# Interleaving the blocks of single experts with the blocks of paired experts in the last stage of a two-layer decoder trunk

## The chip, the cores and the metric

The kernel runs on one core of one Trainium2 chip. The metric is the device time of one execution in microseconds (us). The median of three runs of the kernel before is 1392.48 us (1391.92 to 1393.53).

## The reference, cut to what matters

The kernel computes two decoder layers over 256 tokens of width 1024. The change touches only the last part of the second layer, a mixture of eight experts of which each token uses two:

```python
logits = (x2d @ router).astype(F32)
top_val, top_exp = lax.top_k(logits, 2)          # two of eight experts for each token
gates = jax.nn.softmax(top_val, axis=-1)
...
# for each expert e, on the rows xb of the tokens that chose it:
(jax.nn.silu(xb @ w1[e]) * (xb @ w3[e])) @ w2[e]    # w1, w3: 1024 x 3584, w2: 3584 x 1024, float32
...
# each token sums its two experts' rows times their gates, and then
x = layer_norm(alpha * x + moe(x), ln2_g, ln2_b)
```

The weights of the eight experts are 8 x 3 x 1024 x 3584 floats, 352.3 MB, and each is read from HBM once.

## The kernel before, in words

Up to about 475 us the kernel does the first layer, the attention of the second and the routing. What follows is the stage of the experts, written by `swiglu` from a list of items. The experts are sorted by how many tokens chose them. The first four places (0 to 3) have 128 token slots each and run alone. The last four (4 to 7) have 64 slots each and run in pairs, (4, 5) and (6, 7), the two experts side by side in the two 64-column halves of TensorE.

An item is a block of 512 of the 3584 hidden columns. There are seven items for an expert that runs alone and seven for a pair. An item does the product with w1 (`up` or `up2`), SiLU on ScalarE (line 699), the product with w3, the multiplication of the two on VectorE (line 710), then a transposition (`gate_T`) and the product with w2 (`down`), which is issued in the middle of the next item: after its w1 product and before its w3 product.

- An alone item reads six loads of 1 MB (two each for w1, w3, w2). Each 128x1024 half of a load is split by ScalarE (line 222, `hi`) and VectorE (line 223, `lo`) into two fp32r parts, and each product is three matmuls of 512 columns (`mm3`, lines 232 to 234): 72 matmuls in an item. Five pairs of `hi` and `lo` tiles exist (`WB=5`).
- A pair item reads twelve loads of 1 MB and feeds the raw float32 words to TensorE (line 285 in `up2`, line 650 in `down`). It has no split. The trace has 96 matmul records for an item: 64 for w1 and w3, 32 for w2.

All loads are issued by SyncE's queue (SPq, line 218) in program order, into eleven slots of 1 MB that are used in rotation (`raw()`, the list `late`). A load waits until the readers of the load that had its slot before are done: the VectorE split for an alone item, the matmuls for a pair item. So transfers run at most eleven loads ahead of their use.

The order of the blocks is that of `order` at line 1069: expert 0 alone (seven items), the pair (6, 7), expert 1, expert 2, the pair (4, 5), expert 3. Before an expert's first item its token rows are gathered with one-hot matmuls (`gather` for places that run alone, `gather2` for a pair); places 1 and 2 share one gather. After an expert's last item `combine` (lines 1051 and 1038) scales the result by the gates on ScalarE and VectorE and adds it to the token rows with eight matmuls into `zacc`, four PSUM banks that hold the sums of all tokens for the whole stage. `residual` (line 862) puts alpha times the stage's input into these banks in the third item. PSUM has eight banks here, four tagged `acc` and four tagged `wk`; as `zacc` holds the four `acc` banks, the accumulator of the running expert (`e_acc`, line 1033) holds two of the `wk` banks, and two are left.

`overflow` (line 881) is a branch for experts with more tokens than slots. It is not taken on these inputs, but every engine passes its test, at the second item of place 2. The last item is cut in two of 256 columns.

Of the kernel before, what the change touches and what calls it, by code (L numbers as in the profile page):

```python
# [7 lines left out]
F32 = mybir.dt.float32  # L8
# [5 lines left out]
ALU = mybir.AluOpType  # L14
# [138 lines left out]
def trunk(ctx: ExitStack, tc: tile.TileContext, a, out, R=6, WB=5, NF=16):  # L153
# [60 lines left out]
    def load(w, r0, nr, c0, ncol):  # L214
        t = raw()
        v = t[:, :nr * ncol].rearrange("p (k f) -> p k f", k=nr)
        src = w.at(r0, nr, c0, ncol)
        nc.sync.dma_start(v if len(src.shape) == 3 else t[:, :nr * ncol], src)
        return v
# [70 lines left out]
    def run(*gens):  # L290
        for g in gens:
            yield from g
# [5 lines left out]
    def end(g):  # L298
        for _ in g:
            pass  # L300
# [312 lines left out]

    x1, sta, rest, (behind, _) = finish_ln(accs, x0, g1, b1)

    def swiglu(items, ws, between=None, behind=None, next_ws=None, tail=False):

        def gate_T(it, g):  # L620
            n = it[4]
            if isinstance(it[0], tuple):
                pt, t = wk(), fa("gt")
                for j in range(n // P):
                    TE.transpose(pt[:, j * P:(j + 1) * P], g[0][:, j * P:(j + 1) * P], ident)  # L625
                A.copy(t[:, :n], pt[:, :n])  # L626
                return t
            gs = []
            for q in g:
                pt = wk()  # L630
                for j in range(n // P):
                    TE.transpose(pt[:, j * P:(j + 1) * P], q[:, j * P:(j + 1) * P], ident)  # L632
                gh, gl = fb("gh"), fb("gl")
                A.activation(gh[:, :n], pt[:, :n], AF.Copy)  # L634
                V.tensor_sub(gl[:, :n], pt[:, :n], gh[:, :n].bitcast(F32))  # L635
                gs.append((gh, gl))
            return gs

        def down(it, gs, fill=iter(())):
            w1, w3, w2, c0, n, sta, accs, first, last, pre, post = it  # L640
            nr = n // P
            accs = accs()
            if isinstance(w1, tuple):
                for r in range(0, nr, 2):
                    ws = [load(w, c0 // P + r, 2, 0, D) for w in w2]
                    for j in range(2):
                        for d in range(2):
                            for i, w in enumerate(ws):
                                s = slice((r + j) * P + i * 64, (r + j) * P + (i + 1) * 64)
                                TE.matmul(accs[0][d][i * 64:(i + 1) * 64, :], lhsT=gs[:, s],  # L650
                                          rhs=w[:, j, d * 512:(d + 1) * 512], start=first and r + j == 0,
                                          stop=last and r + j == nr - 1)
                            step(fill)
                end(fill)
                if post:
                    post()
                return
            for r in range(0, nr, 2) if not last else [0]:
                ws = []
                m = 1 if tail and it is items[-1] else 2  # L660
                for q in range(r, nr if last else r + 2, m):
                    v = load(w2, c0 // P + q, m, 0, D)
                    ws += [split(v[:, j:j + 1, :]) for j in range(m)]
                for i, (gh, gl) in enumerate(gs):
                    for d in range(2):
                        for j, (wh, wl) in enumerate(ws):
                            s = slice((r + j) * P, (r + j + 1) * P)
                            c = slice(d * 512, (d + 1) * 512)
                            mm3(accs[i][d], gh[:, s], gl[:, s], wh[:, 0, c], wl[:, 0, c],
                                first and r + j == 0, last and r + j == nr - 1)  # L670
                            step(fill)
            end(fill)
            if post:
                post()

        prev = after = None
        for it in items:
            if it is items[-1] and next_ws:
                after = next_ws()
            w1, w3, w2, c0, n, sta, accs, first, last, pre, post = it  # L680
            fill = pre() if pre else None
            if fill:
                if prev:
                    step(fill, 3)
                    down(prev[0], gate_T(*prev), fill)
                    prev = None
                else:
                    end(fill)
            sta = sta()
            p1 = [wk() for _ in sta]  # L690
            two = isinstance(w1, tuple)
            u = up2(p1[0], w1, c0, n, sta[0]) if two else up(p1, w1, c0, n, sta, ws, between)
            step(u, 2)
            if prev:
                gs = gate_T(*prev)
            end(u)
            s = [fa("sl") for _ in sta]
            for q, p in zip(s, p1):
                A.activation(q[:, :n], p[:, :n], AF.Silu)  # L699
            held = tail and it is items[-1]  # L700
            if prev and not held:
                down(prev[0], gs)
            p3 = [wk() for _ in sta]
            with tc.issue_after(behind) if ws else nullcontext():
                end(up2(p3[0], w3, c0, n, sta[0]) if two else up(p3, w3, c0, n, sta))
            ws = None
            if held:
                down(prev[0], gs)
            for q, p in zip(s, p3):
                V.tensor_mul(q[:, :n], q[:, :n], p[:, :n])  # L710
            prev = (it, s)
        down(prev[0], gate_T(*prev))
        return after and after + next_ws(4)


# [111 lines left out]
    with tc.issue_after(behind):  # L827
# [13 lines left out]
        for h in range(2):  # L841
# [15 lines left out]
            A.activation(t[:, :, 0], gs, AF.Copy)  # L857
            V.tensor_sub(t[:, :, 1], gs, t[:, :, 0].bitcast(F32))
            gg.append(t)
    zacc = [[acc(), acc()] for h in range(2)]  # L860

    def residual():

        identr = fb("identr")[:, :P]
        A.activation(identr, ident, AF.Copy)
        for h in range(2):
            for d in range(2):
                v = x3[:, h, d * 512:(d + 1) * 512]
                hi, lo = fb("xa"), fb("xb")
                A.activation(hi, v, AF.Copy, scale=ALPHA)  # L870
                V.scalar_tensor_tensor(lo, v, ALPHA, hi.bitcast(F32), op0=ALU.mult, op1=ALU.subtract)
                TE.matmul(zacc[h][d], lhsT=identr, rhs=hi, start=True, stop=False)
                TE.matmul(zacc[h][d], lhsT=identr, rhs=lo, start=False, stop=False)

    iota = cst[:, C_IOTA:C_IOTA + P]

# [155 lines left out]

    def e_acc(e):
        if ("acc", e) not in state:
            state["acc", e] = [[wk(), wk()]]
        return state["acc", e]

    def add_up(ys, ot, gs, y, last=False):

        for d in range(2):  # L1040
            c = slice(d * 512, (d + 1) * 512)
            p = ys[d]
            yh, yl = y[:, 0, c], y[:, 1, c]
            A.activation(yh, p, AF.Copy, scale=gs)
            V.scalar_tensor_tensor(yl, p, gs, yh.bitcast(F32), op0=ALU.mult, op1=ALU.subtract)
            for h in range(2):
                s = slice(h * P, (h + 1) * P)
                TE.matmul(zacc[h][d], lhsT=ot[:, s], rhs=yh, start=False, stop=False)  # L1048
                TE.matmul(zacc[h][d], lhsT=ot[:, s], rhs=yl, start=False, stop=last)  # L1049

    def combine(e, last):
        add_up(state["acc", e][0], *state["ot", e], new_y(), last)
# [12 lines left out]

        return [Picked(n, a[n], ROWS[n], at) for n in ("odd_w1", "odd_w3", "odd_w2")]

    items = []
    order = [[0], [6, 7], [1, 2], [2], [4, 5], [3]]
    for j, qs in enumerate(order):  # L1070
        q = qs[0]
        ch = [(c, 512) for c in range(0, D_FFE, 512)]
        if j == len(order) - 1:
            ch[-1:] = [(D_FFE - 512, 256), (D_FFE - 256, 256)]
        ws3 = list(zip(picked(q), picked(q + 1))) if CAP[q] == 64 else picked(q)
        for i, (c, n) in enumerate(ch):
            first, last = i == 0, i == len(ch) - 1
            pre = None
            if first:
                pre = (lambda qs=qs: end(begin(qs))) if q == 2 else lambda qs=qs: begin(qs)  # L1080
            elif (j, i) == (0, 2):
                pre = residual
            elif (j, i) == (3, 1):
                pre = overflow
            items.append((*ws3, c, n, lambda q=q: state["sta", q], lambda q=q: e_acc(q), first, last, pre,
                          (lambda q=q, l=j == len(order) - 1: combine(q, l)) if last else None))
    swiglu(items, ws, behind=behind, tail=True)


    xo = xp.tile([P, 2, D], F32, tag="x", name="xo", bufs=2)  # L1090
# [52 lines left out]
```

## Time and profile before

| What | Before |
|---|---|
| median of three runs | 1392.48 us |
| the profiled execution, its time | 1392.84 us |
| the profiled execution, span from first to last instruction | 1391.2 us |
| TensorE busy over the span | 1301.0 us (94%) |
| VectorE, ScalarE busy | 774.4 us (56%), 618.0 us (44%) |
| bytes read from HBM | 424.03 MB, 306 GB/s over the span |
| granted TensorE clock, mean | 0.986 |

Times in the rows below are microseconds from the start of the span. In a table of stretches each engine has its busy time and, in brackets, the number of its instructions; PEclk is the granted share of TensorE's full clock, and "DMA share" the mean busy share of the sixteen DMA engines. In a timeline the bracket at the end is the idle time of the engine before the row and what ended it. TensorE's busy time is modelled from pipelined matmuls, so a busy TensorE is not always one at full rate: the number of matmuls in a stretch tells more.

### The profile page before, as it was taken

The numbers are of one execution on the slowest core, as the hardware profiler recorded it, in microseconds if no ns is written. First come the engines' busy times: TensorE is split into PE (matmuls) and PEld (weight loads), VectorE is DVE, ScalarE is ACT, GpSimd is POOL, SyncE is SP. The second block draws the span as 40 slices with busy tenths as digits, with TensorE's granted clock in tenths as the row PEclk, the third lists the DMA queues.
The fourth block names the chain that finished last, engine by engine and source line by source line (L and its number), as shares of the span: only waits on it lengthen the run. The fifth ranks groups of instructions, "written<-read, shape, count | busy, mean of one in ns | idle before, by whom it ended". The sixth has DMA issues, their size and how long they took to land. (4 is left out here: it accounts for less than half of the span.)

```text
span 1391.2 us, 16679 instructions
## 1 busy us (share of the span) xinstructions
PE 1301.0 (94%) x6082; PEld 889.5 (64%) x6082; DVE 774.4 (56%) x1190; ACT 618.0 (44%) x866; POOL 53.7 (4%) x40
## 2 busy tenths in 40 slices
PE   9998999999999899999888999989999978799996
PEld 7766888887777788843222378868884322237885
DVE  6987445558777599800000188878882000008897
ACT  5564444534554388710000177777771000007774
POOL 0022000101023000000000000000000000000001
PEclk9999999999999799999999999999999999999998
DMA  9532455645336389969999999979997999999981
GB/s 368 189 124 110 137 202 215 216 178 181 124 149 257 133 336 365 373 280 420 422 421 421 421 421 420 382 279 383 369 371 296 421 421 421 421 421 421 419 300 48
DMA packets 65403, 426.26 MB, mean 306 GB/s; under 512 B 7840, under 2 KB 12192, under 8 KB 15392
## 3 DMA queue, kind: packets, MB, share of 16 engines
q1 hardware_dynamic: 64304, 421.70, 77.1%
q0 software_dynamic: 864, 3.15, 0.6%
q8 instruction: 50, 0.82, 0.2%
q14 instruction: 41, 0.34, 0.1%
q10 hardware_dynamic: 144, 0.26, 0.1%
HBM read 424.03 MB, written 1.05 MB: 306 GB/s over the span
## 5 line engine op out<-in xcount | busy, mean ns | idle before, releaser
L223 DVE TENSOR_TENSOR lo<-raw,hi 128x1024 fp32r<-128x1024 f32 (+2 forms) x462 | 535.2, 1200 | 135.9 <-ACT hi L222 131.1
L222 ACT ACTIVATE hi<-raw 128x1024 fp32r<-128x1024 f32 (+2 forms) x480 | 468.7, 1021 | 189.8 <-PE wk L234 95.0
L285 PE MATMUL wk<-raw,xg 128*64 128x512 f32 x896 | 217.2, 597 | 30.9 <-DMA raw<-in_odd_w 30.9
L710 DVE TENSOR_TENSOR sl<-sl,wk 128x512 f32<-128x512 f32 (+1 forms) x55 | 36.3, 666 | 346.1 <-PE wk L285 318.9
L232 PE MATMUL wk<-hi,xg 128*128 128x512 f32 (+1 forms) x464 | 180.2, 388 | 4.4 <-DVEq L886 4.4
L233 PE MATMUL wk<-lo,xg 128*128 128x512 f32 (+1 forms) x464 | 181.4, 391 | 0.4 <-DVE lo L223 0.4
L234 PE MATMUL wk<-hi,xg 128*128 128x512 f32 (+1 forms) x464 | 179.0, 386 | 0.0
L285 PEld LDWEIGHTS wk<-raw,xg 128*64 128x64 f32 x896 | 66.0, 136 | 157.9 <-issue 101.4
L650 PE MATMUL wk<-raw,gt 128*64 128x512 f32 x448 | 133.5, 602 | 10.1 <-DMA raw<-in_odd_w 8.7
L626 ACT COPY gt<-wk 128x512 f32<-128x512 f32 x14 | 8.2, 585 | 229.0 <-PE wk L625 229.0
L232 PEld LDWEIGHTS wk<-hi,xg 128*128 128x128 f32 x464 | 88.2, 190 | 22.1 <-issue 4.8
L233 PEld LDWEIGHTS wk<-lo,xg 128*128 128x128 f32 x464 | 88.2, 190 | 20.8 <-DVE lo L223 2.2
L234 PEld LDWEIGHTS wk<-hi,xg 128*128 128x128 f32 x464 | 88.2, 190 | 16.6
L699 ACT ACTIVATE sl<-wk 128x512 f32<-128x512 f32 (+1 forms) x55 | 32.0, 582 | 146.7 <-PE wk L285 104.3
L650 PEld LDWEIGHTS wk<-raw,gt 128*64 128x64 f32 x448 | 40.4, 136 | 81.4 <-issue 52.2
L233 PE MATMUL wk<-lo,gh 128*128 128x512 f32 x224 | 87.4, 391 | 0.7 <-DVE lo L223 0.7
L234 PE MATMUL wk<-hi,gl 128*128 128x512 f32 x224 | 87.4, 390 | 0.4 <-DVE gl L635 0.4
L232 PE MATMUL wk<-hi,gh 128*128 128x512 f32 x224 | 82.0, 393 | 0.6 <-ACT gh L634 0.6
L232 PE MATMUL wk<-hi,xT 128*128 128x512 f32 (+1 forms) x192 | 72.3, 377 | 0.3 <-ACT xT L315 0.3
L233 PE MATMUL wk<-lo,xT 128*128 128x512 f32 (+1 forms) x192 | 71.6, 373 | 0.0
L234 PE MATMUL wk<-hi,xT 128*128 128x512 f32 (+1 forms) x192 | 71.5, 373 | 0.0
L232 PE MATMUL acc<-hi,xT 128*128 128x512 f32 (+1 forms) x172 | 68.9, 401 | 0.9 <-ACT xT L315 0.9
(209 smaller groups left out, 1482.7 us busy)
## 6 DMA issues: line engine op xcount, KB each, us to landing
raw<-in_odd_w SPq DMA_DIRECT2D x331, 1024.0 KB, 13.3
raw<-in_even_w SPq DMA_DIRECT2D x31, 1024.0 KB, 4.8
raw<-in_odd_w_in SPq DMA_DIRECT2D x12, 1024.0 KB, 4.8
raw<-in_even_w_in SPq DMA_DIRECT2D x8, 1024.0 KB, 11.9
raw<-in_odd_w SPq DMA_DIRECT2D x10, 512.0 KB, 4.5
raw<-in_even_w_out SPq DMA_DIRECT2D x4, 1024.0 KB, 5.1
raw<-in_odd_w_out SPq DMA_DIRECT2D x4, 1024.0 KB, 4.7
raw<-in_even_w SPq DMA_DIRECT2D x4, 512.0 KB, 3.2
```

The costliest lines, as they stand in the source:

```text
L222: A.activation(hi, v, AF.Copy)
L223: by.tensor_sub(lo, v, hi.bitcast(F32))
L232: TE.matmul(o, lhsT=sh, rhs=wh, start=first, stop=False)
L233: TE.matmul(o, lhsT=sh, rhs=wl, start=False, stop=False)
L234: TE.matmul(o, lhsT=sl, rhs=wh, start=False, stop=last)
L285: TE.matmul(o[i * 64:(i + 1) * 64, :ncol], lhsT=sta(r + k, i), rhs=v[:, k, :], start=r + k == 0, stop=r + k == KT - 1)
L626: A.copy(t[:, :n], pt[:, :n])
L650: TE.matmul(accs[0][d][i * 64:(i + 1) * 64, :], lhsT=gs[:, s], rhs=w[:, j, d * 512:(d + 1) * 512], start=first and r + j == 0, stop=last a ...
L699: A.activation(q[:, :n], p[:, :n], AF.Silu)
L710: V.tensor_mul(q[:, :n], q[:, :n], p[:, :n])
```

## The change

The order of the items is new. The items of the four experts that run alone (28) form one list, those of the two pairs another, first (4, 5), then (6, 7), and the new list takes two of the first and one of the second in turn. Pair items are thus items 3, 6, 9 and so on; the cut item at the end is now that of the pair (6, 7). Each place that runs alone has its own gather. Two experts' accumulators are open at the same time; they take the four `acc` banks, and all four `wk` banks are free for products.

The tokens' sums are no longer in PSUM. `residual` scales the stage's input `x3` in place, with two ScalarE instructions, and a `combine` that is not the last makes its eight matmuls into `wk` banks and adds these to `x3` with four VectorE instructions. In the last product with w2 a new generator `sums` opens four banks (two `acc`, two `wk`) and puts `x3` into them with four float32 matmuls by the identity, and the last `combine` adds to these banks. The final normalization reads them as before. For a pair item that is the very last, `down` loads w2 in pieces of 0.5 MB.

```diff
-    def swiglu(items, ws, between=None, behind=None, next_ws=None, tail=False):
+    def swiglu(items, ws, between=None, behind=None, next_ws=None, tail=None):
...
             if isinstance(w1, tuple):
-                for r in range(0, nr, 2):
-                    ws = [load(w, c0 // P + r, 2, 0, D) for w in w2]
-                    for j in range(2):
+                m = 1 if tail and it is items[-1] else 2
+                for r in range(0, nr, m):
+                    ws = [load(w, c0 // P + r, m, 0, D) for w in w2]
+                    for j in range(m):
...
-        down(prev[0], gate_T(*prev))
+        down(prev[0], gate_T(*prev), *([tail()] if tail else []))
...
-    zacc = [[acc(), acc()] for h in range(2)]
 
     def residual():
 
-        identr = fb("identr")[:, :P]
-        A.activation(identr, ident, AF.Copy)
+        for h in range(2):
+            A.activation(x3[:, h, :], x3[:, h, :], AF.Copy, scale=ALPHA)
+
+    zacc = []
+
+    def sums():
+
+        zacc.extend([[acc(), acc()], [wk(), wk()]])
         for h in range(2):
             for d in range(2):
-                v = x3[:, h, d * 512:(d + 1) * 512]
-                hi, lo = fb("xa"), fb("xb")
-                A.activation(hi, v, AF.Copy, scale=ALPHA)
-                V.scalar_tensor_tensor(lo, v, ALPHA, hi.bitcast(F32), op0=ALU.mult, op1=ALU.subtract)
-                TE.matmul(zacc[h][d], lhsT=identr, rhs=hi, start=True, stop=False)
-                TE.matmul(zacc[h][d], lhsT=identr, rhs=lo, start=False, stop=False)
+                TE.matmul(zacc[h][d], lhsT=ident, rhs=x3[:, h, d * 512:(d + 1) * 512], start=True, stop=False)
+                yield
...
-            state["acc", e] = [[wk(), wk()]]
+            state["acc", e] = [[acc(), acc()]]
...
-                TE.matmul(zacc[h][d], lhsT=ot[:, s], rhs=yh, start=False, stop=False)
-                TE.matmul(zacc[h][d], lhsT=ot[:, s], rhs=yl, start=False, stop=last)
+                ps = zacc[h][d] if last else wk()
+                TE.matmul(ps, lhsT=ot[:, s], rhs=yh, start=not last, stop=False)
+                TE.matmul(ps, lhsT=ot[:, s], rhs=yl, start=False, stop=True)
+                if not last:
+                    V.tensor_add(x3[:, h, c], x3[:, h, c], ps)
...
-    items = []
-    order = [[0], [6, 7], [1, 2], [2], [4, 5], [3]]
-    for j, qs in enumerate(order):
-        q = qs[0]
+
+    def expert(q):
+        end_ = q == 6
         ch = [(c, 512) for c in range(0, D_FFE, 512)]
-        if j == len(order) - 1:
+        if end_:
             ch[-1:] = [(D_FFE - 512, 256), (D_FFE - 256, 256)]
...
             if first:
-                pre = (lambda qs=qs: end(begin(qs))) if q == 2 else lambda qs=qs: begin(qs)
-            elif (j, i) == (0, 2):
+                pre = lambda: begin([q])
+            elif (q, i) == (0, 1):
                 pre = residual
-            elif (j, i) == (3, 1):
+            elif (q, i) == (2, 2):
                 pre = overflow
...
+    alone, paired = run(*(expert(q) for q in range(4))), run(expert(4), expert(6))
+    items = []
+    for it in alone:
+        items += [it, next(alone), next(paired)]
+    items += paired
+    swiglu(items, ws, behind=behind, tail=sums)
```

## Rows read from the trace of the kernel before

**Rows 1.** The page: GB/s in 40 slices of the span.

```profile
GB/s 368 189 124 110 137 202 215 216 178 181 124 149 257 133 336 365 373 280 420 422 421 421 421 421 420 382 279 383 369 371 296 421 421 421 421 421 421 419 300 48
```

**Rows 2.** Stretches: length, engines' busy times, PEclk, DMA share, GB/s.

```profile
480.00:600.00 120.00, 119.34 (x553) 97.78 (x551) 103.36 (x105) 89.19 (x98) 0.00 (x0) 1.00 0.88 332
...
605.00:775.00 170.00, 145.77 (x626) 49.65 (x622) 5.61 (x11) 8.28 (x14) 0.00 (x0) 1.00 1.01 421
800.00:875.00 75.00, 74.60 (x332) 60.36 (x331) 66.07 (x63) 57.34 (x65) 0.00 (x0) 1.00 1.01 420
...
480.00:1360.00 880.00, 821.18 (x3631) 505.66 (x3630) 429.90 (x440) 376.22 (x435) 0.00 (x0) 1.00 0.96 383
```

**Rows 3.** Timeline of VectorE: multiplications of three alone items (start, duration).

```profile
484.19 0.68 DVE L710 TENSOR_TENSOR sl<-sl,wk 128x512 f32<-128x512 f32 x1
...
846.73 0.69 DVE L710 TENSOR_TENSOR sl<-sl,wk 128x512 f32<-128x512 f32 x1 [1.28 <-PE wk L234]
...
863.69 0.69 DVE L710 TENSOR_TENSOR sl<-sl,wk 128x512 f32<-128x512 f32 x1 [1.28 <-PE wk L234]
```

**Rows 4.** The same for the first four items of the first pair.

```profile
614.13 0.69 DVE L710 TENSOR_TENSOR sl<-sl,wk 128x512 f32<-128x512 f32 x1 [15.65 <-PE wk L285]
635.50 0.69 DVE L710 TENSOR_TENSOR sl<-sl,wk 128x512 f32<-128x512 f32 x1 [20.68 <-PE wk L285]
662.50 0.69 DVE L710 TENSOR_TENSOR sl<-sl,wk 128x512 f32<-128x512 f32 x1 [26.31 <-PE wk L285]
692.41 0.69 DVE L710 TENSOR_TENSOR sl<-sl,wk 128x512 f32<-128x512 f32 x1 [29.23 <-PE wk L285]
```

**Rows 5.** Waits from 430 or 475 us on: total us, times, longest.

```profile
SPq L218 <- DVE lo L223: 389.5, 155, 16.5
...
PE wk L285 <- DMA raw<-in_odd_w: 30.9, 24, 1.3
```

**Rows 6.** Loads of the experts' weights: count, size, median us to landing.

```profile
raw<-in_odd_w SPq DMA_DIRECT2D x331, 1024.0 KB, 13.3
...
raw<-in_odd_w SPq DMA_DIRECT2D x10, 512.0 KB, 4.5
```

**Rows 7.** Groups by line from 440 us on: the splits, busy us, mean ns.

```profile
L223 DVE TENSOR_TENSOR lo<-raw,hi 128x1024 fp32r<-128x1024 f32 x324 | 377.6, 1219 | 36.3 <-ACT hi L222 31.8 <-DVEq L886 3.8
L222 ACT ACTIVATE hi<-raw 128x1024 fp32r<-128x1024 f32 x325 | 324.3, 1053 | 43.4 <-PE wk L234 33.6 <-PE acc L234 7.4 <-DVE lo L223 1.5
```

**Rows 8.** Timeline of TensorE where w2 of a pair and a gather alternate.

```profile
788.35 1.08 PE L650 MATMUL wk<-raw,gt 128*64 128x512 f32 x4
...
789.36 0.74 PE L974 MATMUL wk<-oneh,xT 128*128 128x256 f32 x4
...
790.03 1.08 PE L650 MATMUL wk<-raw,gt 128*64 128x512 f32 x4
```

**Rows 9.** VectorE, from expert 2's last item to a pair's first.

```profile
1042.65 0.69 DVE L710 TENSOR_TENSOR sl<-sl,wk 128x512 f32<-128x512 f32 x1 [1.98 <-PE wk L234]
...
1070.57 0.69 DVE L710 TENSOR_TENSOR sl<-sl,wk 128x512 f32<-128x512 f32 x1 [15.65 <-PE wk L285]
```

**Rows 10.** VectorE, expert 1 to expert 2, then past the branch.

```profile
915.18 0.69 DVE L710 TENSOR_TENSOR sl<-sl,wk 128x512 f32<-128x512 f32 x1 [0.60 <-PE wk L234]
...
934.07 0.69 DVE L710 TENSOR_TENSOR sl<-sl,wk 128x512 f32<-128x512 f32 x1 [0.73 <-PE wk L234]
...
957.13 0.69 DVE L710 TENSOR_TENSOR sl<-sl,wk 128x512 f32<-128x512 f32 x1 [2.35 <-PE wk L234]
```

**Rows 11.** From a pair's multiplication to its w2 product; the last combine's first step.

```profile
782.02 0.69 DVE L710 TENSOR_TENSOR sl<-sl,wk 128x512 f32<-128x512 f32 x1 [8.77 <-PE wk L285]
...
784.15 1.07 PE L650 MATMUL wk<-raw,gt 128*64 128x512 f32 x2 [0.73 <-ACT gt L626]
...
1377.28 1.37 ACT L1044 ACTIVATE y<-wk,gs 128x512 fp32r<-128x512 f32 x2 [3.01 <-PE wk L234]
```

**Rows 12.** A stretch with the 0.5 MB loads.

```profile
1352.00:1354.00 2.00, 2.00 (x14) 1.80 (x13) 1.39 (x4) 1.27 (x2) 0.00 (x0) 1.00 0.94 291
```

More of the change, by code (lines that the diff above doesn't have):

```diff
@@ L1079, in trunk @@
             if first:
-                pre = (lambda qs=qs: end(begin(qs))) if q == 2 else lambda qs=qs: begin(qs)
-            elif (j, i) == (0, 2):
+                pre = lambda: begin([q])
+            elif (q, i) == (0, 1):
                 pre = residual
-            elif (j, i) == (3, 1):
+            elif (q, i) == (2, 2):
                 pre = overflow
-            items.append((*ws3, c, n, lambda q=q: state["sta", q], lambda q=q: e_acc(q), first, last, pre,
-                          (lambda q=q, l=j == len(order) - 1: combine(q, l)) if last else None))
-    swiglu(items, ws, behind=behind, tail=True)
+            yield (*ws3, c, n, lambda: state["sta", q], lambda: e_acc(q), first, last, pre,
+                   (lambda: combine(q, end_)) if last else None)
+    alone, paired = run(*(expert(q) for q in range(4))), run(expert(4), expert(6))
[4 more added lines that the diff above has]
+    swiglu(items, ws, behind=behind, tail=sums)
     xo = xp.tile([P, 2, D], F32, tag="x", name="xo", bufs=2)
```

## The prediction

> **What bounds the kernel now.** I read the page's GB/s line first [rows 1]: in the stage of the experts (slices 14 to 39) it alternates between plateaus at 421 and stretches of 270 to 380. The table of stretches says why [rows 2]. In the pair stage (605 to 775) transfers run at 421 GB/s with a DMA share of 1.01, while TensorE has 626 matmul records in 170 us, 3.7 per us. In the alone stages it is the other way: from 480 to 600 TensorE is busy 119.3 of 120 us, and transfers make only 332 GB/s. So the two kinds of item have different limits, and each stage leaves idle what the other lacks. Over 480 to 1360 us transfers average 383 GB/s.
>
> The items' cadence gives the sizes. An alone item takes 16.96 us (863.69 - 846.73 [rows 3]), of which 72 matmuls at 75 us / 332 = 0.226 us (800 to 875 [rows 2]) are 16.3; its six loads, 6.29 MB, are 14.9 us of transfer at 421. A pair item takes 21.4 us as long as its data are there (first to second multiplication [rows 4]); its twelve loads, 12.58 MB, take 29.9 us, and that is the cadence after a few items (third to fourth [rows 4]). Two alone and one pair item together: TensorE 2 x 16.9 + 21.4 = 55.2 us, transfers 25.17 MB / 421 = 59.8 us. The whole stage is 331 loads of 1 MB and 10 of half that [rows 6], 352.3 MB or 837 us at 421, and TensorE's 14 groups are 773 us and its extras: nearly equal totals, which now lie partly one behind the other.
>
> What keeps them from overlapping today is the reach of eleven slots: SyncE's queue waits 389.5 us for splits to free a slot, and TensorE waits for loads in the pair stages [rows 5]. In the first pair stage, items one and two keep 21.4 us and the third loses 5.6 [rows 4]. By the third multiplication, 662.5, two items and the eight w1 and w3 loads of the third are used, 33.6 MB, and 421 GB/s from 605 on gave 24.2 MB: the lead was 9.4 MB, 22 us of transfer. That is short against a block of seven pair items, but long against one.
>
> **The change part by part.** I sum TensorE's path, from the first alone item's multiplication at 484.2 us [rows 3], where both orders are alike, to the end, and then test it against the transfers.
>
> (1) Items. 27 more alone items x 16.9 = 456 us; 13 pair items x 21.4 = 278; the two halves of the cut one 21. What is removed is the waiting of the pair items: some 8.5 us (29.9 - 21.4) in five items of each block.
>
> (2) Changes of form. TensorE now goes between 128-column fp32r and 64-column float32 work about eight times in three items, where a pair item has two today (its transposition). The row that shows one: four pair records take 1.01 us and four 256-column gather matmuls 0.67 us until the next kind starts [rows 8]; at 0.2155 us per 512 columns they would be 0.86 and 0.43, so two changes cost 0.39 us. Six more changes in each of 14 groups at 0.2 us are 17 us. The Trainium skill, "TensorEngine Tiling (Array Packing)", Key Properties, says against this change that switching the tiling mode drains TensorE; it has no price, and rows 8 are what such a drain costs here.
>
> (3) Gathers and combines. The step from an alone expert to a pair took 27.9 us [rows 9]. Its w2 product with transposition (5.9) and the pair's w1 and w3 (64 records, 13.8) are 19.7 of it; the rest, with 0.7 lost in the item before, is 8.9 us for a gather and a combine. A combine between two alone experts cost 18.9 - 17.0 = 1.9 us [rows 10]; I take 2.5 (bounds 1.9 and 3.4) and 5.5 for a gather with its slot matrix. Behind the anchor there are now five gathers (four before: places 1 and 2 shared one), 27.5 us, and five combines ahead of the tail, 12.5. The branch costs 23.1 - 17.0 = 6.1 us [rows 10], as before. Together 46 us.
>
> (4) Sums in SBUF. The eight matmuls of a combine stay. New are four VectorE additions of 128x512, 0.69 us each by the multiplication of that shape [rows 3], 2.8 us in each of five combines; each waits for two matmuls, and behind it on VectorE wait the splits. An alone item has 12 splits of 1.22 us [rows 7] and two smaller steps, 16.0 us in 16.9, so there is little room, but five split pairs are in stock. Bounds 0 and 14 us; I take 3, because pair items give VectorE its room back. As `x3` stays in use, one buffer instead of two is left for `y`; combines lie an item or more apart, so the matmuls that hold it are done and it costs nothing, or one combine's 2.5 us where two experts end in one group. `residual` loses eight matmuls and four VectorE steps that lie behind the anchor; counting it at 0 is safe, as its two ScalarE scalings of 1.05 us [rows 7] fit beside TensorE.
>
> (5) Waits at seams. Where an alone piece follows a pair piece, its first split may not be ready: ScalarE 1.05 and VectorE 1.22 us [rows 7], 2.3 us, at three such seams in each group, 42 in all. Bounds 0 and 96 us. Between alone items, where splits run ahead, an item takes 16.96 us against 72 x 0.226 + 0.5 = 16.8, so 0.1 to 0.2 us is lost; ScalarE and VectorE idle in the pair stages (8.3 and 5.6 us of 170 [rows 2]), so splits should be ahead here too. I take 0.1 us, 4 us.
>
> (6) Tail. After the last multiplication come the way to the w2 product (2.1 us in a whole item [rows 11], 1.5 in a half one), 16 records x 0.2155 = 3.4 us, and the four identity matmuls of `sums`. No such float32 matmul is in the trace; between a fp32r one (0.226) and the four records of a float32 pair that fill the same array (0.86) I take the upper, 3.4 us. From the last combine's first step to the end it stays 1391.2 - 1377.3 = 13.9 us [rows 11], and 0.6 for a change of form.
>
> Sum: 484 + 456 + 278 + 21 + 17 + 46 + 3 + 4 + 1.5 + 3.4 + 3.4 + 0.6 + 13.9 = 1332 us. I round down by 2, as the first items after the anchor ran at 16.8 us: 1330 of span. The profiled execution was 1.6 us longer than its span and 0.4 above the median, so 1331 us.
>
> **Do the transfers keep up?** From 480 to 1360 us 880 x 0.383 = 337.0 MB moved [rows 2], nearly all that was left. At 421 that is 800 us. The first two items and a gather leave the slots full and cost some 9 us; the pieces of 0.5 MB at the end (20, 10.5 MB) move at 291 to 421 [rows 12], up to 10 us more. So transfers end at 1290 to 1300, 30 us ahead of the end, and alone would give about 1315. The lead, 22 us of transfer at the first pair, falls by 59.8 - 55.2 - 1.2 = 3.4 us a group, and gathers, combines and the branch refill it. Before the seventh pair it is thinnest: 22 - 6 x 3.4 + 8 (expert 1's gather and combine) = 9.6 us. Within a group the pair's three pieces draw 6.5 us, so 3 us are left. TensorE paces, narrowly.
>
> **The rivals.** (A) Seams cost about 0.8 us each, a third of what they can: 42 x 0.8 = 34 instead of 4, thus 1361. For it: two streams share five split pairs and two in-order engines, and SiLU and the copies of a pair stand in the same queues. Against it: before, the splits ran ahead past just such steps.
>
> (B) Slower. ScalarE and VectorE are kept in the order in which the items are written: the splits for an alone w2 product stand behind the pair item's SiLU, which waits for its w1 matmuls, and those for w1 and w3 behind its copy and multiplication. Then each of the 42 seams shows the full 2.3 us: 96 instead of 4, thus 1423. From 1.6 us a seam on ((1391 - 1326) / 42) the change loses. Speaking against: TensorE's pace of 0.226 us holds over whole alone stages.
>
> (C) Transfers pace: TensorE's extras hide in the wait for data, 1315 as worked out above.
>
> (D) It gains nothing. Either the lead is worth less than 22 us, and each of the 14 pair items still waits 4.3 us more (60 us), or transfers do not hold 421 for 800 us: 383 GB/s, today's mean, gives 880 us and 1391. Against both: 420 and 421 held in a pair and in an alone stage [rows 2]. The Trainium skill, "SBUF — State Buffer", Summary, would have HBM transfers counted at about 358 GB/s; by that the 337 MB take 941 us, and the end is past 1430. Rows 2 show 421 for 170 us on end, so I give it next to nothing.
>
> **How the numbers follow.** Forecast (1318 to 1345) 55%, A (1345 to 1385) 21%, C (1305 to 1318) 12%, B 7%, D 5%. The forecast is the likeliest: 1331. From 1312 on, most of C is in; up to 1366, the nearer half of A: together a little over 8 in 10. A difference of 0.2%, 2.8 us, is about what a measurement tells from none. Faster: all of the forecast and of C, A, a part of D: 0.89. Same: 0.04. Slower: B, with a little of D: 0.07.
>
> **What would show it.** In stretches of 60 us between 500 and 1280, both sides should be full: DMA share near 1.0 and some 250 matmul records. From every third multiplication to the next it should be 56 to 58 us; TensorE's wait for loads (30.9 us at line 285 now [rows 5]) should nearly go. If a group takes 59.8 us and the share is 1.01 all through, C holds. If TensorE idles behind line 223 or 222 at the seams, it is A or B, by its length. If it still idles for loads with the share below 1, the lead is too short (D). The prediction falls if the cadence of alone or pair items is not 16.9 and 21.4 when they are mixed.

## The result and the profile after

The change takes 1378.46 us, the median of four runs (1374.65 to 1378.92), against 1392.33 before: a ratio of 0.9893 (95% interval 0.9874 to 0.9912). It is faster by 1%, 14 us where 61 were forecast, and outside the range. The profiled execution is the fastest of the four, 1374.65 us with a span of 1372.9.

The page of after, GB/s in 40 slices, and two stretches of it (columns as in [rows 2]): the first group of two alone items and a pair item, from one pair's multiplication to the next, and a later one.

```profile
GB/s 371 193 101 103 166 184 218 221 194 162 155 151 176 170 308 396 422 420 421 412 375 421 419 420 409 381 362 226 420 421 412 405 411 344 421 415 418 394 234 167
...
525.00:581.00 56.00, 56.00 (x253) 34.50 (x253) 29.41 (x27) 28.04 (x30) 0.00 (x0) 1.00 0.99 409
1033.00:1094.00 61.00, 57.98 (x253) 35.15 (x252) 30.97 (x30) 26.66 (x30) 0.00 (x0) 1.00 1.01 412
```

The valleys of [rows 1] are mostly gone (the deepest left, 226, lies at the branch), and the pair's waits for data too. TensorE's list of waits for loads at line 285 had 30.9 us on matmuls (PE, [rows 5]) and this on weight loads (PEld):

```profile
PEld wk L285 <- DMA raw<-in_odd_w: 53.6, 33, 2.2
```

Of the loads of the experts only the first row below is left in it; the others are the loads' own waits for slots:

```profile
PEld wk L285 <- DMA raw<-in_odd_w: 2.0, 6, 0.4
...
SPq L218 <- DVE lo L223: 337.3, 132, 11.6
SPq L218 <- PE wk L285: 221.4, 73, 10.3
SPq L218 <- PE acc L651: 104.3, 26, 8.9
```

So the change does what it says: pairs and singles share the transfers. But the two groups above hold the same 253 matmul records, and the first takes 56.0 us with TensorE never idle, the second 61.0 with 3.0 us idle; the other 2.0 us stand in records that the model of busy time draws out. The granted clock is 1.00 in both. The multiplications on VectorE (start, duration) show where. The first two rows bound the first group, the last four are a later one:

```profile
525.12 0.69 DVE L711 TENSOR_TENSOR sl<-sl,wk 128x512 f32<-128x512 f32 x1 [12.37 <-PE wk L285]
...
581.11 0.69 DVE L711 TENSOR_TENSOR sl<-sl,wk 128x512 f32<-128x512 f32 x1 [8.13 <-PE wk L285]
...
1032.76 0.69 DVE L711 TENSOR_TENSOR sl<-sl,wk 128x512 f32<-128x512 f32 x1 [9.03 <-PE wk L285]
1052.90 0.69 DVE L711 TENSOR_TENSOR sl<-sl,wk 128x512 f32<-128x512 f32 x1 [5.39 <-PE wk L234]
1069.89 0.69 DVE L711 TENSOR_TENSOR sl<-sl,wk 128x512 f32<-128x512 f32 x1 [2.44 <-PE wk L234]
1093.76 0.69 DVE L711 TENSOR_TENSOR sl<-sl,wk 128x512 f32<-128x512 f32 x1 [9.06 <-PE wk L285]
```

From pair to pair it is 56.0 us at first (forecast 56.4), and 61.0 in later groups that hold no gather, combine or branch, called steady below: 20.1 for the alone item behind the pair, 17.0 for the second, 23.9 for the pair item. Such a step ends with an item's multiplication, so it holds the item's w1 and w3 products and the w2 product of the item before: only the sum of the three compares with the forecast's. Three engines around the start of that pair item's w2 stretch, the seam from a pair piece to an alone piece:

```profile
1069.89 0.69 DVE L711 TENSOR_TENSOR sl<-sl,wk 128x512 f32<-128x512 f32 x1 [2.44 <-PE wk L234]
1072.11 0.69 DVE L635 TENSOR_TENSOR gl<-wk,gh 128x512 fp32r<-128x512 f32 x1 [1.53 <-ACT gh L634]
1080.07 4.63 DVE L223 TENSOR_TENSOR lo<-raw,hi 128x1024 fp32r<-128x1024 f32 x4 [7.26 <-ACT hi L222]
...
1071.48 0.60 ACT L634 ACTIVATE gh<-wk 128x512 fp32r<-128x512 f32 x1 [6.23 <-PE wk L632]
1078.49 0.60 ACT L700 ACTIVATE sl<-wk 128x512 f32<-128x512 f32 x1 [6.41 <-PE wk L285]
1078.98 5.79 ACT L222 ACTIVATE hi<-raw 128x1024 fp32r<-128x1024 f32 x6
...
1072.71 5.74 PE L285 MATMUL wk<-raw,xg 128*64 128x512 f32 x24
1080.09 0.73 PE L232 MATMUL acc<-hi,gh 128*128 128x512 f32 x2 [1.63 <-ACT hi L222]
1081.35 0.50 PE L233 MATMUL acc<-lo,gh 128*128 128x512 f32 x1 [0.53 <-DVE lo L223]
```

ScalarE idles 6.41 us with the SiLU of line 700 at its head, which waits for the pair's w1 product; the alone item's w2 splits stand behind it. When SiLU has started at 1078.49, `hi` follows at 1078.98, `lo` at 1080.07, and TensorE has nothing to do from the end of the pair's product until then. In the first group it is otherwise: three `lo` stand right behind the alone item's multiplication, 7 us ahead of SiLU:

```profile
560.64 0.69 DVE L711 TENSOR_TENSOR sl<-sl,wk 128x512 f32<-128x512 f32 x1 [2.67 <-PE wk L234]
561.24 3.49 DVE L223 TENSOR_TENSOR lo<-raw,hi 128x1024 fp32r<-128x1024 f32 x3
...
568.43 0.60 ACT L700 ACTIVATE sl<-wk 128x512 f32<-128x512 f32 x1 [3.02 <-PE wk L285]
```

The second kind of seam is from the pair's w3 product to the next alone item's w1. There `hi` is ready, but `lo` stands behind the pair's multiplication on VectorE, and the transposition waits for that multiplication too:

```profile
1032.62 0.50 PE L232 MATMUL wk<-hi,xg 128*128 128x512 f32 x1
1033.50 0.66 PE L625 MATMUL wk<-cst,sl 128*128 128x128 f32 x4 [0.39 <-DVE sl L711]
1034.63 0.50 PE L233 MATMUL wk<-lo,xg 128*128 128x512 f32 x1 [0.48 <-DVE lo L223]
...
1033.36 4.77 DVE L223 TENSOR_TENSOR lo<-raw,hi 128x1024 fp32r<-128x1024 f32 x4
```

### The profile page after: what moved, and what is told of

It reads as the page before. It is cut to its first block, busy times and chain, and to the rows that moved or that the text cites. A ratio compares the mean times of both kernels' runs of the same rounds, so it can differ in the third digit from the quotient of the medians.

```text
span 1372.9 us, 16689 instructions
## 1 busy us (share of the span) xinstructions
PE 1301.1 (95%) x6130; PEld 887.7 (65%) x6130; DVE 784.9 (57%) x1201; ACT 614.4 (45%) x859; POOL 53.7 (4%) x40
## 5 line engine op out<-in xcount | busy, mean ns | idle before, releaser
L223 DVE TENSOR_TENSOR lo<-raw,hi 128x1024 fp32r<-128x1024 f32 (+1 forms) x454 | 535.2, 1220 | 244.1 <-ACT hi L222 237.3
L285 PE MATMUL wk<-raw,xg 128*64 128x512 f32 (+1 forms) x960 | 210.3, 568 | 0.2
L232 PE MATMUL wk<-hi,xg 128*128 128x512 f32 x448 | 179.3, 401 | 7.1 <-DVEq L888 6.6
L233 PE MATMUL wk<-lo,xg 128*128 128x512 f32 x448 | 178.4, 398 | 5.0 <-DVE lo L223 5.0
L234 PE MATMUL wk<-hi,xg 128*128 128x512 f32 x448 | 175.6, 392 | 0.0
L232 PE MATMUL acc<-hi,gh 128*128 128x512 f32 x312 | 119.1, 401 | 15.1 <-ACT hi L222 14.5
L233 PE MATMUL acc<-lo,gh 128*128 128x512 f32 x312 | 123.3, 397 | 4.8 <-DVE lo L223 4.8
L234 PE MATMUL acc<-hi,gl 128*128 128x512 f32 x312 | 122.1, 394 | 1.4 <-DVE gl L635 1.2
L651 PE MATMUL acc<-raw,gt 128*64 128x512 f32 x448 | 100.9, 598 | 0.3 <-ACT gt L626 0.3
L232 PEld LDWEIGHTS acc<-hi,gh 128*128 128x128 f32 x312 | 58.3, 189 | 36.6 <-ACT hi L222 22.0
L233 PEld LDWEIGHTS acc<-lo,gh 128*128 128x128 f32 x312 | 59.1, 189 | 21.7 <-DVE lo L223 9.4
L232 PE MATMUL wk<-hi,xT 128*128 128x512 f32 (+1 forms) x192 | 72.6, 378 | 0.3 <-ACT xT L315 0.3
```

The source lines that it names most:

```text
L223: by.tensor_sub(lo, v, hi.bitcast(F32))
L232: TE.matmul(o, lhsT=sh, rhs=wh, start=first, stop=False)
L233: TE.matmul(o, lhsT=sh, rhs=wl, start=False, stop=False)
L234: TE.matmul(o, lhsT=sl, rhs=wh, start=False, stop=last)
L285: TE.matmul(o[i * 64:(i + 1) * 64, :ncol], lhsT=sta(r + k, i), rhs=v[:, k, :], start=r + k == 0, stop=r + k == KT - 1)
```

## The experiments

Theory G: the 5 us that a later group loses is TensorE waiting at seams, because a split stands behind a step on ScalarE or VectorE that itself waits for TensorE. Rival C: a group is set by its loads, 25.17 MB or 59.8 us at 421 GB/s. Much speaks for C: in the later group above the share of the DMA engines is 1.01 and the time 61.0 us, close to the forecast's own sign for it (59.8 us and a share of 1.01 all through). By C, an edit that leaves the loads as they are changes nothing.

In the table, p is a pair item, a' the alone item behind it, a the next one, by the multiplications of a steady group; us.

| Kernel | p | a' | a | group | median of all |
|---|---|---|---|---|---|
| the change | 23.9 | 20.1 | 17.0 | 61.0 | 1378.46 |
| transpositions held (e1) | 23.0 | 20.6 | 17.5 | 61.1 | 1378.32 |
| splits first (e2) | 21.4 | 20.2 | 17.0 | 58.6 | 1352.20 |
| both (e3) | 20.5 | 20.6 | 17.5 | 58.6 | 1356.37 |
| all seams (e5) | 20.5 | 18.8 | 17.5 | 56.8 | 1339.33 |

**e1, transpositions held.** In the first group the transpositions stand in the middle of a w1 product, in later ones behind its first matmul. This edit puts them in the middle everywhere; `newest` is the w1 matmul issued last, noted in `mm3` and `up2`.

```diff
...
-                gs = gate_T(*prev)
+                with tc.issue_after(newest[0]) if tail else nullcontext():
+                    gs = gate_T(*prev)
```

> Only the place of the transpositions in TensorE's order changes: each stands behind the first half of the next item's w1 product, as in the text, instead of behind its first one or two matmuls as in most groups of the changed kernel. Theory G (the order fixed at build time makes TensorE wait for other engines at the seams, though data are there): the piece 'first alone matmul, four transpositions, 23 matmuls' falls from 7.4 to about 6.1 us and the pair's from 8.0 to 7.75, 1.6 us in each of some 9 groups, so 12 to 17 us less than the changed kernel: about 1362. Theory C (transfers pace the groups, the seams only fill their wait): no change, 1374 to 1379, as each group still takes about 61 us.

Measured: 1378.32 us (ratio to the kernel before 0.9900, 0.9883 to 0.9916), no gain over the change: a miss for G, which gave 1362, and taken alone it spoke for C. But the wait had only moved, from the transposition to the next split, which stands behind the pair's multiplication:

```profile
1035.91 0.50 PE L234 MATMUL wk<-hi,xg 128*128 128x512 f32 x1
1037.93 0.50 PE L235 MATMUL wk<-lo,xg 128*128 128x512 f32 x1 [1.52 <-DVE lo L223]
```

**e2, splits first.** The four w2 splits of the alone item are written ahead of the pair's SiLU, which is queued behind the newest `hi` (noted in `parts`).

```diff
...
-            for q, p in zip(s, p1):
-                A.activation(q[:, :n], p[:, :n], AF.Silu)
+            ready = None
+            if tail and two and prev and not isinstance(prev[0][0], tuple):
+                ready = []
+                for r in range(0, prev[0][4] // P, 2):
+                    v = load(prev[0][2], prev[0][3] // P + r, 2, 0, D)
+                    ready += [split(v[:, j:j + 1, :]) for j in range(2)]
+            with tc.issue_after(newest_hi[0]) if ready else nullcontext():
+                for q, p in zip(s, p1):
+                    A.activation(q[:, :n], p[:, :n], AF.Silu)
...
-                down(prev[0], gs)
+                down(prev[0], gs, ready=ready)
```

> Only ScalarE's order changes: in a pair item the four splits for the w2 product of the alone item before it are queued ahead of the pair's SiLU. Theory G: the gap of 1.6 us ahead of that w2 product and the slow start behind it (0.85 us) go, 2.4 us in each of some 10 groups: about 24 us less than the changed kernel, 1353. Theory C: no change, 1374 to 1379.

Measured: 1352.20 us (0.9715, 0.9699 to 0.9731), 26 less, as G gave it. The same seam, ScalarE and then TensorE:

```profile
1059.83 3.88 ACT L224 ACTIVATE hi<-raw 128x1024 fp32r<-128x1024 f32 x4
1066.35 0.60 ACT L711 ACTIVATE sl<-wk 128x512 f32<-128x512 f32 x1 [2.63 <-PE wk L287]
...
1065.29 1.02 PE L287 MATMUL wk<-raw,xg 128*64 128x512 f32 x2
1066.24 0.73 PE L234 MATMUL acc<-hi,gh 128*128 128x512 f32 x2
```

Four `hi` run before SiLU, and TensorE goes over without idling. The pair item falls from 23.9 to 21.4 us, and groups of 58.6 follow one another, below the 59.8 us of their loads. Two such groups could still draw on loads that had landed ahead; but the order of ScalarE alone, with the same loads, gave 26 us, and so C falls.

**e3, the edits of e1 and e2 together.**

> Both edits. Theory G: groups fall from 61.0 to about 56 us, as in the first group of the changed kernel, and the time to about 1337, if the loads that have landed ahead (12 to 19 us before their use) are enough to bridge. Theory C: groups cannot go below 59.8 us (25.17 MB at 421 GB/s), so at most 1.2 us a group, 1360 or more.

Measured: 1356.37 us (0.9737, 0.9720 to 0.9753). A miss for G: with the transpositions held, p falls to 20.5, but a' stays at 20.6. The second kind of seam was still there, since its `lo` waits behind the pair's multiplication whether or not the transposition does.

**e5, all seams.** On top of e3, the first two w1 splits of the next alone item are taken ahead of the pair's multiplication; `then` is the next item of the list, and `up` goes on from `begun`.

```diff
...
-            for q, p in zip(s, p3):
-                V.tensor_mul(q[:, :n], q[:, :n], p[:, :n])
+            then = items[at + 1] if at + 1 < len(items) else None
+            if tail and two and then and not isinstance(then[0], tuple) and not then[9]:
+                g = pieces(then[0], then[3], then[4], 2)
+                begun = run([next(g), next(g)], g)
+            with tc.issue_after(newest_lo[0]) if begun else nullcontext():
+                for q, p in zip(s, p3):
+                    V.tensor_mul(q[:, :n], q[:, :n], p[:, :n])
```

> The changed kernel with all three seams of a group eased: the w2 splits queued ahead of the pair's SiLU, the two transpositions held until half of the next w1 product is issued, and the first two w1 splits of the next alone item taken ahead of the pair's multiplication on ScalarE and VectorE. Theory (what a steady group loses over the first one, 61.0 against 56.0 us, is TensorE waiting at the seams for splits that stand behind another step on ScalarE or VectorE): groups of 56 to 56.5 us throughout, 2.3 us less than with the splits alone (58.6) in about ten groups, so 1352 - 25 = 1327 us (1322 to 1335). Rival (transfers set the floor of a group): never below 59.8 us for long, waits for loads come up in TensorE's list, 1340 to 1352 us. Rival (the change of form itself costs more in a steady group): still 58.6, 1350 us.

Measured: 1339.33 us (0.9613, 0.9597 to 0.9629), the fastest kernel of all, but 12 us above what G gave and outside its range: a group lost 1.8 us where 2.3 were expected, and groups with a gather or a combine gained little. The time alone nearly suits the rival of the transfers, but its mechanism is not there: groups of 56.8 us follow one another, and of TensorE's waits for loads 0.6 us are left. The rival of the changes of form, by which groups stay at 58.6, falls with that too. The a' item is at 18.8: twelve matmuls in a row, the transposition, and no wait (the first two, the transposition and the matmul behind it are shown, and what is left of waits for loads).

```profile
1072.01 0.50 PE L236 MATMUL wk<-hi,xg 128*128 128x512 f32 x1
1072.35 0.40 PE L237 MATMUL wk<-lo,xg 128*128 128x512 f32 x1
...
1074.87 0.60 PE L629 MATMUL wk<-cst,sl 128*128 128x128 f32 x4
1075.22 0.48 PE L236 MATMUL wk<-hi,xg 128*128 128x512 f32 x1
...
PEld wk L289 <- DMA raw<-in_odd_w: 0.6, 2, 0.4
```

**e6, blocks of four and two,** a test of the seams by their number, on the changed kernel.

```diff
-        items += [it, next(alone), next(paired)]
+        items += [it, *(next(alone) for _ in range(3)), next(paired), next(paired)]
```

> The changed kernel with blocks of four alone items and two pair items instead of two and one: half as many seams, no other edit. Theory of the seams: four alone and two pair items take 23.85 + 21.4 + 20.1 + 3 x 17.0 = 116.4 us where two groups take 122.0; 5.6 us less in six of seven blocks, so 1378 - 34 = 1344 us (1338 to 1352). Rival (transfers set a group's 61 us): no change, 1374 to 1380. Rival (the lead of the loads is short): a second pair item on end draws 9 us more of it and waits for its data, so 1380 to 1400.

Measured: 1351.57 us (0.9702, 0.9685 to 0.9718): 27 of the 34 us that G gave. The last pair item of a block takes 22.2 instead of 21.4, and ScalarE's waits for loads rise from 7.5 to 61.0 us, so the lead of the loads over their use is drawn on.

**e7, four and two with the splits first** (the edits of e2 and e6 together).

> Blocks of four and two, and the w2 splits of the last alone item queued ahead of the pair's SiLU. Theory of the seams: 21.4 + 21.4 + 20.2 + 3 x 17.0 = 114.0 us for a block where two groups with the splits first take 117.2; 1352 - 20 = 1332 us (1326 to 1340). Rival (a group of 58.6 is set by transfers at 59.8): no better than 1352. Rival (lead short): TensorE waits for loads in the second pair item of a block.

Measured: 1341.97 us (0.9637, 0.9621 to 0.9653). That is 10 us below e2, half of what G gave; behind the first block the second pair items take 22.2 to 24.2 us, and 29.3 at the branch. **e10** has the edits of e5 in blocks of four and two:

> All seams eased, in blocks of four and two. Theory (with the seams eased, only the changes of form are left of a group's cost, and blocks halve the number at the ends of pieces): 1 to 2 us less in each of seven blocks, 1327 to 1334 us. Rival (the second pair item on end overtakes its loads, 421 GB/s being the limit there): waits for loads in TensorE's list, 1337 to 1350 us.

Measured: 1340.95 us (0.9629, 0.9613 to 0.9645), the rival's outcome: no better than two and one. One pair item stands at 26.8 us where ScalarE waited 15.3 us for a load; in all ScalarE waits 89.0 us for loads (38.2 in e5) and TensorE's matmuls 2.5. With the seams eased the blocks gain nothing; that the lead is now the limit fits these waits, but was not tested by itself.

**e8 and e9, nine slots** instead of eleven from the start of the experts on, in the changed kernel and in e5.

```diff
-    late += ["raw"] * 4 + ["qT", "kT", "vv", "oh", "ol"] + ["raw"] * (R - 4) + ["x"]
+    late += ["raw"] * 4 + ["qT", "kT", "vv"] + ["raw"] * (R - 4) + ["x"]
```

> The changed kernel with nine slots for loads behind the start of the experts instead of eleven, no other edit: 2.1 MB, 5 us of transfer, less of lead. Theory of the seams: loads land 12 to 19 us ahead of their use, so nothing is lost, 1374 to 1382 us. Rival (loads are late and pace the group): each of 14 groups loses up to 5 us, 1400 to 1450 us.

Measured: 1381.69 us (0.9919, 0.9903 to 0.9936), 3.2 more than with eleven (the two profiled executions lie 6.6 apart, as that of the change is its fastest). Steady groups stay at 61.0; the difference of the profiles lies in the first groups (58.5 and 61.0 instead of 56.0 and 59.7) and around the branch (72.6 and 70.7 instead of 71.0 and 68.5). Loads do not pace the changed kernel.

> The kernel with all three seams eased, with nine slots for loads instead of eleven. It runs its groups in 56.8 us where a group's loads take 59.8 at 421 GB/s, so it lives on the lead. Theory (the lead of about 22 us is drawn down by some 3 us a group and is thin, as the forecast had it, so 5 us less of it shows): TensorE waits for loads in the later groups of each stretch, groups go from 56.8 towards 59.8, 1345 to 1360 us. Rival (the lead is never used up): no change, 1336 to 1342 us.

Measured: 1349.18 us (0.9689, 0.9672 to 0.9705), 10 more than e5, as the theory gave. Groups are 56.8 where the lead holds and 58.2 to 59.5 where it has run out. ScalarE's waits for loads, first in e5 and then here (total, times, longest):

```profile
ACT hi L224 <- DMA raw<-in_odd_w: 38.2, 22, 6.9
```

```profile
ACT hi L224 <- DMA raw<-in_odd_w: 141.2, 63, 9.9
```

**e4, the sums alone.** The old order of blocks with the sums in SBUF, the new banks and a gather for each place. The cut item is again expert 3's, and the branch stands where it stood.

```diff
...
-    alone, paired = run(*(expert(q) for q in range(4))), run(expert(4), expert(6))
-    items = []
-    for it in alone:
-        items += [it, next(alone), next(paired)]
-    items += paired
+    items = list(run(*(expert(q) for q in (0, 6, 1, 2, 4, 3))))
```

> One part of the change alone: the sums are kept in SBUF, the accumulators take the banks that this frees, each place has its own gather, and the blocks run in the old order (expert 0, pair, 1, 2, pair, 3). The prediction's steps say nearly nothing: an own gather for place 2 instead of a shared one +2 us where the blocks of alone experts meet, additions 0 to 3 us, the eight matmuls of the residual step -2: within 4 us of the kernel before, 1388 to 1396. The rival is that the additions on VectorE hold up splits: 2.8 us for each of five combines, up to 1406.

Measured: 1396.24 us (1.0026, 1.0014 to 1.0037), 3.5 more than the 1392.70 of the kernel before in the same series, at the upper end of what was expected and 10 below the rival's bound. That is the price of all preparations together, the extra gather included; they are not told apart.

## Why the prediction missed

**The step that failed is (5), the waits at seams.** It took 0.1 us a seam, 4 us in all, on the ground that ScalarE and VectorE idle in the pair stages, so that splits would be ahead. They do idle, but with an instruction at the head of their order that waits for TensorE (ScalarE 6.41 us before SiLU at 1078.49), and the splits behind it do not start; with the splits put ahead (e2) they run in that time. So idle time of these two engines was room only for what stood at the head of their order. Measured by what each edit gave back, a steady group loses about 2.5 us at the seam pair to alone w2 (23.9 against 21.4, e2) and 1.3 at the seam to alone w1 behind the multiplication (20.1 against 18.8, e5). The transpositions give another 0.9 in the pair item and cost 0.5 in the second alone item; in all 61.0 - 56.8 = 4.2 us, or 1.4 for each of the three seams that the forecast counted. The third of these, from the pair's w2 to the alone item's w3, costs nothing: TensorE goes over without idling (line 232 behind line 651, in the group that starts at 1033):

```profile
1046.12 1.08 PE L651 MATMUL acc<-raw,gt 128*64 128x512 f32 x4
1047.13 0.50 PE L232 MATMUL wk<-hi,xg 128*128 128x512 f32 x1
```

Over the groups from 525 us to the last pair item, the profiled run of the change takes 813.7 us and that of e5 778.3: 35.4 of the 43 us by which the span missed 1330, 0.9 us for each of the 39 seams in these 13 groups.

**The rivals.** What the runs show is B's mechanism: splits behind the pair item's SiLU, and those for w1 behind its multiplication, with about B's price (2.3 us) at the first of the three. B's time, 1423, came out too high because the third seam costs nothing and the second not the whole price, the first group has another order, and groups with a gather or a combine lose little (65.1 against 63.7 us with the seams eased). The time fell into A's range, 1345 to 1385; A had the size and B the cause. The reason set against both, that splits ran ahead of such steps over whole alone stages, was read rightly but did not carry over. There, too, SiLU waits for TensorE at the head of ScalarE's order, but two of the four w2 splits stand ahead of it, and the w2 product starts before SiLU does (kernel before):

```profile
1338.88 2.00 ACT L222 ACTIVATE hi<-raw 128x1024 fp32r<-128x1024 f32 x2
1342.22 0.62 PE L232 MATMUL wk<-hi,gh 128*128 128x512 f32 x2
1342.42 0.60 ACT L699 ACTIVATE sl<-wk 128x512 f32<-128x512 f32 x1 [1.54 <-PE wk L234]
```

In the steady groups of the change none stands ahead of the pair's SiLU: between `gh` at 1071.48 and SiLU at 1078.49 ScalarE has no split. Why the built order differs from seam to seam is not shown by the runs. With 0.9 us a seam on the average the change stays below B's break-even of 1.6, and keeps 14 us.

**What held.** (1) and (2): 56.0 us in the first group and 56.8 in e5 against 56.4. (3) and (4): in e5 the five groups with gathers, combines and the branch take 6.9, 4.5, 14.2, 11.1 and 6.9 us more than 56.8, together 43.6; the forecast's terms for these four gathers, four combines with sums and one branch are 4 x 5.5 + 4 x 3.1 + 6.1 = 40.5. Part of the rest lies at the branch: in e5 TensorE idles 7.1 us there instead of 4.4 before, and over the next 5 us of its work the granted clock is 0.50 (955.4 to 960.4 us; the lower of its two levels, 1.2 GHz) instead of 0.66 before (938.4 to 943.4). With the seams eased, the whole missed by 7.6 us (span 1337.6 against 1330).

(6) came out near, 23.8 us from the last multiplication to the end against 22.8, but by luck. The four identity matmuls are eight records, about 0.9 us a matmul, so the upper bound taken (3.4 us for four) was right as a price; but half of them ran ahead of the last multiplication. In their place the w2 product behind it has 32 records where 16 were counted, since that of the first half item is issued there too:

```profile
1346.00 1.13 PE L874 MATMUL acc<-x,cst 128*128 128x512 f32 x2
1349.87 1.88 PE L874 MATMUL wk<-x,cst 128*128 128x512 f32 x4
1351.68 7.14 PE L651 MATMUL acc<-raw,gt 128*64 128x512 f32 x32
```

**The transfers.** "TensorE paces, narrowly" was right: in e5 it does with eleven slots and no longer does with nine. It leaves little beyond e5: from 525 to 1300 us e5 moves 409 GB/s at a DMA share of 1.00, against 398 and 0.97 in the change. Transfers ran at 421 GB/s over whole slices, as [rows 2] had it, so D's 383 GB/s was a result of the old order. The Trainium skill, "Perfetto Trace Analysis", Roofline, gives the limit of one core that is alone on its memory as its sixteen DMA engines, about 435 GB/s; the 421 here agrees with that and not with the 358 that was weighed in the prediction.

## What to carry to other kernels

Where two streams are mixed on engines that each have a fixed order of work, don't count an engine's idle time as cover: look in the trace at which instruction stands at its head while it idles, and what is queued behind it. If it waits for the engine that the split or copy is meant to feed, price each seam in full, and then move the feeding work ahead of it; here three such moves turned 14 us of gain into 54. A DMA share near 1.0 does not show by itself that loads pace: at 1.01 the change lost 3 us by nine slots instead of eleven, and gained 26 by another order of splits. Fewer slots, or a faster consumer, tells the two apart.

## What was not expected

A group can run faster than its loads, 56.8 us against 59.8 at 421 GB/s, and so do the eight groups of e5 without a gather, combine or branch. Gathers, combines and the branch, in which TensorE does other work, give the loads time to get ahead again; that this is what refills the lead is argued from e9, where groups slow to 58.2 to 59.5 with two slots fewer. And removing one wait of two that stand close together gave nothing (e1, 1378.32 against 1378.46), and together with e2 even lost (1356.37 against 1352.20), while the same edit is part of the best kernel: held transpositions cost half a microsecond in each alone item (17.5 against 17.0), and what they give shows only when the split behind them is early as well. Whether e5 without them would be faster still was not tried.
